# Row pairs 14 and 15 first in two of seven block products, their base kept in SBUF, and 40 accumulating DMAs spaced four products apart

## The chip, the cores and the metric

The kernel runs on one core of a Trainium2 chip. The core has a matrix engine (TensorE, PE in the profile, with its weight loads PEld), a vector engine (VectorE, DVE), a scalar engine (ScalarE, ACT), GpSimd (POOL) and a sync engine (SyncE, SP). In this kernel SP, ACT and POOL also issue DMAs. The metric is the device time of one execution in microseconds. Lower is better.

## The reference

The operation is a soft mixture of experts: every token goes through all eight experts, and the results are summed with the weights of a softmax.

```python
x [16, 512, 512]; router_logits [16, 512, 8]; expert_weights [8, 512, 2048]   # float32
probs = softmax(router_logits, axis=-1)
output = sum over e of probs[:, :, e:e+1] * (x @ expert_weights[e])           # [16, 512, 2048]
```

Seen as one matrix product, the left side has 8192 rows (tokens) and 4096 columns (expert times hidden, each already multiplied by its probability), and the right side is 4096 by 2048.

## The kernel before, in words

**Two levels of seven products.** The big product is cut 2 by 2 and done with seven block products P1 to P7 instead of eight (Winograd's form of Strassen's scheme). The 8192 rows are cut into 32 blocks of 256 rows. Row pair q (0 to 15) is the blocks 2q and 2q+1, one from each half of the scheme. For one row pair, one such product is 256 rows by 2048 by 1024, and it is again done by seven steps in the order 1, 5, 6, 2, 7, 3, 4 (`STEPS`), each of eight 128x128x512 matmuls. Some stages cut part of this a third time (`by_thirds`, `by_twos`), with 128x256 matmuls. The result of a product is four tiles of 128x512 float32, 256 KB each, named by (row half, column half).

**What is written where.** For row pair q the output has four blocks: C11 (even rows, left columns), C12 (even rows, right columns), C21 and C22 (odd rows).

- P1 goes to a DRAM scratch `kept[q]`. P2 goes to C11. For ten of the row pairs P1 is added onto C11 later by `add_kept`: four DMAs of 256 KB from `kept` to the output with an add, 40 in all, issued by POOL.
- P5 goes to C21. P6 starts from a base, P1 minus P5: `kept[q]` is fetched into SBUF tiles and P5's tiles are subtracted there (`joined`). P6 adds to the base in place and the tiles go to C12.
- P7 starts from what P6 left, adds in place, and goes to C22. Its base is fetched back from C12 in DRAM into SBUF (class `Base`, `fetch`, issued by SP).
- P4 starts from P7's tiles in SBUF and is added onto C21 by accumulating DMAs. P3 is added onto C12 in the same way.

All writes from a product's tiles to the output are DMAs issued by POOL (`pool`, line 121).

**The tiles that matter here.** Every 128x512 float32 tile outside PSUM comes from one pool, `hpool`, with 12 buffers (tiles named `h`). A new `h` tile takes the buffer whose last use in program order lies furthest back, and the first instruction that writes it waits until that use is over. If the last use is a write to the output, this means the landing of that DMA.

**Stages.** Work is listed in stages of one or two products, worked through step by step, alternating between the two: first product step 1, second product step 1, first product step 5, and so on. A stage of two has 14 slots. Stages 0 to 6 are P1, 7 to 14 are P2, 15 to 30 are P5 and P6, 31 (`k7`) is P6 of pair 15 with P7 of pair 0, 32 to 46 are P4 of pair q with P7 of pair q+1, 47 (`k3`) is P4 of pair 15 with P3 of pair 14, 48 to 54 are two P3 each and done by thirds, 55 is the last P3. `products[4, 15].apart` makes the last P4 write to new `h` tiles instead of in place.

**The order is written by hand.** Hooks `at(stage, slot, ...)` place loads, weight preparation, base fetches and `add_kept` at slots. Vector work that prepares later stages waits in a queue with costs, and a small planner (`slack`, `need`) takes it out between matmul groups. The resulting program order is kept on each engine, so an instruction that has to wait holds up all that follow on its engine or queue. POOL issues its DMAs in program order as well.

**Where the weights turn over.** Around stage 31 the weights of P4 and P7, around stage 47 the weights of P3 are fetched from DRAM scratch (`fetch_w`, issued by ACT, 1 MB each). From stage 47 on, P3 also loads a stored left side of 1 MB for each row pair (`ZBlock`, issued by SP).

The base fetches of P7 and the accumulating DMAs are placed by these lines:

```python
for slot, tn in zip((7, 9, 11, 17) if q else (10, 12, 14, 17), INNER):      # line 995, for each q
    fetch_at(k7 + q - 1 + slot // 14, slot % 14, bases[7, q], tn)
for n, q in enumerate(q for q in range(ON_BASE) if q not in WITH_KEPT):     # line 1246
    for i in range(4):
        at(*slots_after(k7 + 3, 0, 20 * n + 5 * i), lambda q=q, i=i: add_kept(q, i // 2, i % 2))
```

Of the kernel before, what the change touches and what calls it, by code (L numbers as in the profile page):

```python
# [31 lines left out]
def kernel(  # L32
# [87 lines left out]
    def pool(o, i, **how):  # L120
        note(nc.gpsimd.dma_start(out=o, in_=i, **how))  # L121
# [252 lines left out]
    def need(task):  # L374
        if task is not None and not task.done:
            flush(task)
            clock["pe"] = max(clock["pe"], clock["dve"])
# [275 lines left out]


    KEPT_Z = 14
    ND = 7
    ON_BASE = 14
    WITH_KEPT = (5, 1, 7, 9)

    def out_rows(q, odd, cols, tn):  # L660
        t, n = tn
        return out_f[ds((2 * q + odd) * HQ + t * HP, HP), ds(cols * NH + n * NB, NB)]

    def to_out(q, odd, cols, **how):
        return lambda tn, o: pool(out_rows(q, odd, cols, tn), o, **how)
# [14 lines left out]
    INNER = ((0, 0), (1, 1), (0, 1), (1, 0))  # L680
# [5 lines left out]
    def at(stage, slot, make):  # L686
        hooks.setdefault((stage, slot), []).append(make)

    def add(*products):
        stages.append(products)  # L690
        return len(stages) - 1
# [4 lines left out]
    lefts, xs, ps_, bases = {}, {}, {}, {}  # L696

    def xblock(h):
        if h not in xs:
            xs[h] = XBlock(h)  # L700
        return xs[h]

    def left_of(r, q, fresh=True):
        a, b = 2 * q, 2 * q + 1
        if r == 1:
            pt = PBlock(a, P1, xp1[q - 2][1] if q in (2, 3) else None)
            if q in (2, 3):
                xs[a] = XBlock(a, xp1[q - 2][0])
            return Left(xblock(a), pt), [xblock(a), pt]
        if r in (2, 4):  # L710
            h, pt = (a, PBlock(a, P2)) if r == 2 else (b, PBlock(b, P2))
            return Left(xblock(h), pt), [xblock(h), pt]
        if r == 5:
            pt = PBlock(b, PQ)
            return Left(xblock(b), pt), [xblock(b), pt]
        if r == 6:
            pt = PBlock(a, P1)
            return Left(xblock(a), pt, of=lefts[5, q]), [xblock(a), pt]
        if r == 3 and q < KEPT_Z:
            pt, kept_z = PBlock(a, P2), ZBlock(q)  # L720
            return Left(xblock(a), pt, kept=kept_z), [xblock(a), pt, kept_z]
        pa, pb = PBlock(a, P1 if r == 7 else PQ), PBlock(b, P1 if r == 7 else PQ)
        return Left(xblock(a), pa, (xblock(b), pb)), [xblock(a), pa, xblock(b), pb]

    def kept_rows(q):
        return lambda tn: kept[q][tn[1], ds(tn[0] * HP, HP), :]

    def product(r, q, **how):
        left, loads = left_of(r, q)
        lefts[r, q] = left  # L730
        p = None
        if r == 1:
            def sink(tn, o):
                pool(kept_rows(q)(tn), o)
            p = Product(right[1], left, sink)
        elif r == 2:
            if q >= ON_BASE or q in WITH_KEPT:
                bases[2, q] = Base(kept_rows(q))
            p = Product(right[2], left, to_out(q, 0, 0), bases.get((2, q)))
        elif r == 5:  # L740
            bases[6, q] = m1 = Base(kept_rows(q))
            m1.task = {}

            p = Product(right[5], left, to_out(q, 1, 0))
        elif r == 6:
            m1 = bases[6, q]

            def base(tn):
                need(m1.task[tn])
                return m1.t[tn]  # L750
            p = Product(right[6], left, to_out(q, 0, 1), base)
        elif r == 7:
            base = bases[7, q] = Base(lambda tn: out_rows(q, 0, 1, tn))
            p = Product(right[7], left, to_out(q, 1, 1), base)
        elif r == 4:
            p = Product(right[4], left, to_out(q, 1, 0, accum_op=ADD), products[7, q].o.__getitem__)
        else:
            p = Product(right[3], left, to_out(q, 0, 1, accum_op=ADD), **how)
        p.loads = loads
        products[r, q] = p  # L760
        return p

    products = {}
# [179 lines left out]
    def fetch_at(stage, slot, base, *tns):  # L943
        for tn in tns:
            at(stage, slot, lambda tn=tn: base.fetch(tn))


    for q in range(2, 16, 2):
        add(product(1, q), product(1, q + 1))
    xs.clear()  # L950
    for q in (2, 4, 0, 6, 8, 10, 12, 14):
        add(product(2, q), product(2, q + 1))
    for q in (*WITH_KEPT, *range(ON_BASE, 16)):
# [3 lines left out]
        fetch_at(k, 3, bases[2, q], INNER[3])  # L957
    xs.clear()
    k5 = add(product(5, 0), product(5, 1))
    add(product(6, 0))  # L960
    for q in range(1, 15):
        add(product(6, q), product(5, q + 1))
    some = product(6, 15)
    xs.clear()
    k7 = add(some, product(7, 0))
    for q in range(15):
        add(product(4, q), product(7, q + 1))
    some = product(4, 15)
    xs.clear()
    k3 = add(some, product(3, KEPT_Z))  # L970
    for q in range(0, KEPT_Z, 2):
        add(product(3, q), product(3, q + 1))
# [1 line left out]
    late[k3 - 1] = 6  # L974
    late[k3] = 10
    late[k7] = 12
    products[4, 15].apart = True

    def claim(of, tn):
        of[tn] = half()  # L980
# [2 lines left out]
    def joined(q, tn):  # L983
        m1 = bases[6, q]
        m1.task[tn] = later(0.69, lambda: tt(m1.t[tn], m1.t[tn], products[5, q].o[tn], SUB), True)

    for q in range(16):
        k = k5 + 1 + q
        duo = len(stages[k - 1]) == 2
        for slot, tn in zip((2, 4, 6, 8) if duo else (1, 2, 3, 4), INNER):  # L990
            fetch_at(k - 1, slot, bases[6, q], tn)
        for tn, where in zip(INNER, ((k - 1, 12), (k - 1, 13), (k - 1, 13), (k, 3)) if duo
                             else ((k - 1, 5), (k - 1, 6), (k - 1, 6), (k, 3))):
            at(*where, lambda q=q, tn=tn: joined(q, tn))
        for slot, tn in zip((7, 9, 11, 17) if q else (10, 12, 14, 17), INNER):
            fetch_at(k7 + q - 1 + slot // 14, slot % 14, bases[7, q], tn)


    def wedge(kn, e):

# [26 lines left out]
    def wedge_at(stage, slot, kn, e, then):  # L1027
        made = []

        def begin():  # L1030
            casts, made_ = wedge(kn, e)
            casts()
            made.extend(made_)

        def go_on():
            for make in made:
                later(1.22, make)
        at(stage, slot, begin)
        at(*then, go_on)
# [9 lines left out]
    def sums_at(stage, slot, r, of, ps, first=False):  # L1049
        def go():  # L1050
            if right[r].w is None:
                right[r].sums = right[r].build(of)
            for p in ps:
                right[r].queue_sum(right[r].sums, p, first)
        at(stage, slot, go)
    sums_at(ND - 1, 5, 2, b21, (5,))
    sums_at(ND - 1, 7, 2, b21, (6,))
    sums_at(ND - 1, 9, 2, b21, (7,))
    sums_at(ND - 1, 12, 2, b21, (4,))
    ODD = 0, 1  # L1060
    for i, (kn, e) in enumerate((kn, e) for kn in (ODD, (0, 0), (1, 1), (1, 0)) for e in range(2)):
        stage = ND + i - 2 if kn != ODD else 2 + 2 * i
        wedge_at(stage, 2, kn, e, (stage + 1, 0))
# [41 lines left out]
    def slots_after(stage, slot, n):  # L1105
        slot += n
        while slot >= 7 * len(stages[stage]):
            slot -= 7 * len(stages[stage])
            stage += 1
        return stage, slot  # L1110
# [97 lines left out]

    for q in range(KEPT_Z):
        z_dram[q] = dram.tile([P, 2 * K8, HQ], f16, name=f"z_{q}")  # L1210
# [15 lines left out]
    def third_at(stage, slot, of, r, p):  # L1226
        def make():
            of[p] = third_sums(right[r].w[p])
        at(stage, slot, lambda: later(2.76, make))
    third_at(1, 5, third, 1, 2)  # L1230
    for stage in range(2, ND - 1):
        twos[stage] = Twos(*(p.left for p in stages[stage]), third)
# [10 lines left out]
    def add_kept(q, n, t):  # L1243
        pool(out_f[ds(2 * q * HQ + t * HP, HP), ds(n * NB, NB)], kept[q][n, ds(t * HP, HP), :], accum_op=ADD)

    for n, q in enumerate(q for q in range(ON_BASE) if q not in WITH_KEPT):
        for i in range(4):
            at(*slots_after(k7 + 3, 0, 20 * n + 5 * i), lambda q=q, i=i: add_kept(q, i // 2, i % 2))

    finish = products[3, 15]  # L1250
    finish.base = Base(lambda tn: out_rows(15, 0, 1, tn))
# [81 lines left out]
```

## Time and profile before

| what | value |
|---|---|
| median of 3 runs | 1365.92 us (1365.02 to 1368.73) |
| the profiled execution's own time | 1368.37 us |
| its span, first to last instruction | 1366.6 us |
| PE busy | 1352.8 us (99%) |
| DVE busy | 1156.6 us (85%) |
| ACT busy, POOL busy | 254.0 us, 422.3 us |
| DMAs `out_dram<-h` (results to the output, POOL) | 380 of 256 KB |
| DMAs `out_dram<-kept` (P1 onto C11, POOL) | 40 of 256 KB |
| DMAs `h<-out_dram` (bases read back, SP) | 68 of 256 KB |

How to read it: tiles are named by what they hold, `ps` and `pt` are PSUM banks, `h` the 128x512 float32 tiles, `w` the weights and the stored left sides, `z` and `d` left sides. `out_dram<-h` means a transfer or instruction that writes `out_dram` and reads `h`. Line L121 is the helper that issues POOL's DMAs, L118 that of SP, L130 the matmul helper, L107 the helper of all two-input vector operations, so tiles tell more than lines. L624, L628, L632, L645 and L831 to L847 are ScalarE copies out of PSUM. A busy PE is not PE at its peak: when the granted clock (PEclk) is 0.50, matmuls take twice as long and still count as busy.

### The profile page before, as it was taken

How to read it: one execution, taken by the hardware profiler on the slowest of the kernel's cores; microseconds unless marked ns; L12 is line 12 of the kernel's file. 1: busy time of each engine (PE TensorE's matmuls, PEld its weight loads, DVE VectorE, ACT ScalarE, POOL GpSimd, SP SyncE). 2: the span in 40 equal slices, each digit the busy share in tenths (PEclk: the TensorE clock that was granted, in tenths of full speed). 3: DMA queues.
4: the chain of work that ended last, by engine and by line, in shares of the span. 5: the costliest groups of instructions: out<-in, count | busy, mean ns of one | idle time of the engine just before them, and what ended most of it. 6: DMA issues, size and time to landing. Idle time of an engine off the chain costs nothing.

```text
span 1366.6 us, 18926 instructions
## 1 busy us (share of the span) xinstructions
PE 1352.8 (99%) x6894; PEld 672.1 (49%) x6894; DVE 1156.6 (85%) x1426; ACT 254.0 (19%) x517; POOL 422.3 (31%) x651
## 2 busy tenths in 40 slices
PE   9999999999999999999999999999999999989998
PEld 4566655565544444444444444444444444546564
DVE  7878898888999888887878899898888987868886
ACT  3233323232211111111111100000000000223331
POOL 3223322323222323223221122433534433232232
PEclk9999999999999999999999999999999999999999
DMA  9999979998999999999987997999999999999986
GB/s 184 245 216 242 263 244 233 307 297 258 272 321 280 304 296 284 280 272 308 290 276 278 361 305 196 279 233 260 238 240 239 274 243 309 325 276 220 209 130 119
DMA packets 191117, 355.67 MB, mean 260 GB/s; under 512 B 53040, under 2 KB 81968, under 8 KB 186160
## 3 DMA queue, kind: packets, MB, share of 16 engines
q0 software_dynamic: 87520, 185.12, 57.9%
q1 hardware_dynamic: 99760, 144.05, 34.5%
q10 hardware_dynamic: 3744, 25.30, 4.7%
q8 instruction: 54, 0.88, 0.3%
q14 instruction: 39, 0.32, 0.1%
HBM read 210.53 MB, written 176.36 MB: 283 GB/s over the span
## 4 chain that ended last, share of the span: by engine, by line
PE 77%; issue 10%; DMA 8%; POOL 3%; DVE 1%; ACT 0%; POOLq 0%; DVEq 0%; SPq 0%; ACTq 0%
PE ps L130 59%; PE pt L130 18%; DMA out_dram<-h 4%; POOL out_dram L121 2%; DMA w<-in_expert_weights_dram 1%; DMA out_dram<-kept 1%; DMA h<-out_dram 1%; DMA wd<-w 1%; POOL wd L121 0%; DVE h L107 0%; DVE z L107 0%; DVE w L107 0%; POOL w L121 0%; POOL xs L121 0%; DVE u L107 0%
## 5 line engine op out<-in xcount | busy, mean ns | idle before, releaser
L130 PE MATMUL ps<-w,z 128*128 128x512 f16 (+1 forms) x3728 | 811.5, 374 | 2.1 <-DVE h L107 0.9
L130 PEld LDWEIGHTS <-z 128*128 128x128 f16 x5312 | 520.0, 98 | 572.5 <-issue 2.6
L121 POOL DMA_DIRECT2D out_dram<-h x380 | 251.2, 687 | 702.0 <-ACT h L645 282.6
L130 PE MATMUL pt<-w,z 128*128 128x512 f16 (+1 forms) x1584 | 325.6, 352 | 0.3 <-DMA w<-in_expert_weights_dram 0.3
L107 DVE TENSOR_TENSOR z<-xT,pT 128x2048 f16<-128x2048 f16 x220 | 265.6, 1216 | 0.8 <-DMA xT<-xs 0.8
L107 DVE TENSOR_TENSOR h<-ps,h 128x512 f32<-128x512 f32 x270 | 183.9, 687 | 79.1 <-PE ps L130 60.7
L130 PE MATMUL ps<-w,d 128*128 128x512 f16 x880 | 199.7, 379 | 0.0
L130 PEld LDWEIGHTS <-d 128*128 128x128 f16 x880 | 86.1, 98 | 98.9
L632 ACT COPY h<-ps 128x512 f32<-128x512 f32 x102 | 59.8, 586 | 396.8 <-PE ps L130 359.5
L107 DVE TENSOR_TENSOR z<-z,d 128x2048 f16<-128x2048 f16 x110 | 132.3, 1216 | 0.0
L107 DVE TENSOR_TENSOR h<-pt,h 128x512 f32<-128x512 f32 x123 | 83.5, 686 | 43.5 <-PE pt L130 41.6
L107 DVE TENSOR_TENSOR w<-w 128x1024 f16<-128x1024 f16 (+2 forms) x108 | 112.7, 1059 | 0.8
L645 ACT COPY h<-ps 128x512 f32<-128x512 f32 x54 | 31.7, 586 | 398.5 <-PE ps L130 397.4
L107 DVE TENSOR_TENSOR d<-z 128x1024 f16<-128x1024 f16 x110 | 73.9, 684 | 0.9
L628 ACT COPY h<-ps 128x512 f32<-128x512 f32 x89 | 50.0, 598 | 76.7 <-PE ps L130 74.6
L107 DVE TENSOR_TENSOR ps<-ps,h 128x512 f32<-128x512 f32 (+1 forms) x70 | 44.3, 636 | 21.5 <-PE ps L130 16.0
L121 POOL DMA_DIRECT2D kept<-h x56 | 30.7, 548 | 87.0 <-DVE h L107 48.0
L624 ACT COPY ps<-ps 128x512 f32<-128x512 f32 x47 | 26.8, 570 | 110.4 <-PE ps L130 51.0
L107 DVE TENSOR_TENSOR z<-z 128x2048 f16<-128x2048 f16 (+1 forms) x48 | 45.6, 957 | 1.4
L107 DVE TENSOR_TENSOR h<-h 128x512 f32<-128x512 f32 (+2 forms) x69 | 45.1, 674 | 1.1 <-DMA h<-kept 0.9
L107 DVE TENSOR_TENSOR z<-z,u 128x2048 f16<-128x2048 f16 x36 | 44.1, 1225 | 1.2
L107 DVE TENSOR_TENSOR u<-xT,pT 128x2048 f16<-128x2048 f16 x36 | 43.8, 1217 | 0.0
(83 smaller groups left out, 553.8 us busy)
## 6 DMA issues: line engine op xcount, KB each, us to landing
out_dram<-h POOLq DMA_DIRECT2D x380, 256.0 KB, 7.2
pT<-p_dram SPq DMA_DIRECT2D x126, 256.0 KB, 7.2
w<-wd ACTq DMA_DIRECT2D x23, 1024.0 KB, 10.2
h<-kept SPq DMA_DIRECT2D x88, 256.0 KB, 7.4
xT<-x SPq DMA_DIRECT2D x80, 256.0 KB, 7.1
h<-out_dram SPq DMA_DIRECT2D x68, 256.0 KB, 5.9
w<-in_expert_weights_dram POOLq DMA_DIRECT2D x33, 512.0 KB, 11.0
kept<-h POOLq DMA_DIRECT2D x56, 256.0 KB, 6.8
```

The lines of the kernel that those rows point to most:

```text
L107: dve(nc.vector.tensor_tensor(out=o, in0=a, in1=b, op=op))
L121: note(nc.gpsimd.dma_start(out=o, in_=i, **how))
L130: note(nc.tensor.matmul(ps, z, w, start=start, stop=stop, skip_group_check=True))
L624: act(nc.scalar.copy(self.banks["b"], x))
L628: act(nc.scalar.copy(o[tn], q if p == 5 else x))
L632: act(nc.scalar.copy(o[TN[p]], b if p == 2 else x))
L645: act(nc.scalar.copy(o[tn], b))
```

## The change

Three things change.

1. P7 and P4 take the row pairs in the order 14, 15, 0, 1, ..., 13 instead of 0 to 15. Stage 31 is now P6 of pair 15 with P7 of pair 14, stage 32 P4 of pair 14 with P7 of pair 15, stage 33 P4 of pair 15 with P7 of pair 0, and stage 47 P4 of pair 13 with P3 of pair 14.
2. For pairs 14 and 15, P7 takes P6's own four tiles in SBUF as its base and adds to them in place. The eight fetches from C12 that would bring these bases are gone. The other 14 pairs fetch their base as before, at the same slots before their use. The four special slots that pair 0 had (10, 12, 14, 17) are gone.
3. The 40 accumulating DMAs of `add_kept` begin at the same place (stage 34, slot 0) and follow each other 4 slots apart instead of 5. The last one is at slot 156 counted from there (stage 45, slot 2) instead of slot 195 (stage 47, slot 13).

```diff
+    ORDER_7 = (14, 15, *range(14))
...
         elif r == 7:
-            base = bases[7, q] = Base(lambda tn: out_rows(q, 0, 1, tn))
+            base = products[6, q].o.__getitem__
+            if q not in ORDER_7[:2]:
+                base = bases[7, q] = Base(lambda tn: out_rows(q, 0, 1, tn))
...
-    k7 = add(some, product(7, 0))
-    for q in range(15):
-        add(product(4, q), product(7, q + 1))
-    some = product(4, 15)
+    k7 = add(some, product(7, ORDER_7[0]))
+    for q, then in zip(ORDER_7, ORDER_7[1:]):
+        add(product(4, q), product(7, then))
+    some = product(4, ORDER_7[-1])
...
-    products[4, 15].apart = True
+    products[4, ORDER_7[-1]].apart = True
...
-        for slot, tn in zip((7, 9, 11, 17) if q else (10, 12, 14, 17), INNER):
-            fetch_at(k7 + q - 1 + slot // 14, slot % 14, bases[7, q], tn)
-
+    for n, q in enumerate(ORDER_7[2:], 2):
+        for slot, tn in zip((7, 9, 11, 17), INNER):
+            fetch_at(k7 + n - 1 + slot // 14, slot % 14, bases[7, q], tn)
...
-            at(*slots_after(k7 + 3, 0, 20 * n + 5 * i), lambda q=q, i=i: add_kept(q, i // 2, i % 2))
+            at(*slots_after(k7 + 3, 0, 16 * n + 4 * i), lambda q=q, i=i: add_kept(q, i // 2, i % 2))
```

## The prediction, written before the changed kernel was run

> **What bounds the kernel now.** I read the busy times first, then who PE waits for, then the stages in which it waits, and last what ends those waits.
>
> ```profile
> span 1366.6 us, 18926 instructions
> PE 1352.8 (99%) x6894; PEld 672.1 (49%) x6894; DVE 1156.6 (85%) x1426; ACT 254.0 (19%) x517; POOL 422.3 (31%) x651
> ```
>
> PE is busy 99% of the span and the change leaves every matmul in place. So time can only come from PE's idle gaps and from matmuls run at a lower clock, or be lost to new gaps. The waits of PE:
>
> ```profile
> PE pt L130 <- ACT h L835: 4.3, 1, 4.3
> ...
> PE ps L130 <- DVE h L107: 0.9, 1, 0.9
> PE ps L130 <- ACT h L628: 0.7, 1, 0.7
> PE ps L130 <- DVE z L107: 0.5, 1, 0.5
> PE pt L130 <- ACT ps L831: 0.4, 1, 0.4
> ```
>
> The waits left out here belong to the kernel's first microseconds, which the change does not touch. The stages in which the five fall, one row per stage (window, its length, then busy time per engine, the granted clock, the DMA share and GB/s):
>
> ```profile
> 766.48:791.74 25.26, 24.35 (x113) 10.92 (x112) 21.63 (x24) 1.76 (x3) 3.78 (x7) 1.00 0.98 368
> 791.74:816.38 24.64, 24.17 (x113) 10.82 (x112) 23.65 (x28) 1.17 (x2) 5.37 (x9) 1.00 0.85 271
> 816.38:1106.40 290.02, 290.02 (x1345) 131.46 (x1344) 258.08 (x308) 14.07 (x24) 114.38 (x161) 1.00 0.98 247
> 1179.17:1203.93 24.76, 23.70 (x137) 13.29 (x136) 20.24 (x26) 8.16 (x18) 6.62 (x9) 1.00 1.08 302
> 1203.93:1233.49 29.56, 25.21 (x137) 14.17 (x136) 19.71 (x25) 8.04 (x18) 10.34 (x13) 0.94 1.09 256
> 1233.49:1256.87 23.38, 23.38 (x137) 13.29 (x136) 19.64 (x25) 8.23 (x18) 6.84 (x9) 1.00 1.00 228
> 1212.29:1215.71 3.42, 3.42 (x19) 2.44 (x17) 0.87 (x2) 0.85 (x2) 0.53 (x1) 0.50 1.06 252
> ```
>
> The first two rows are stages 31 and 32, where P7 begins: PE idles 25.26 - 24.35 = 0.91 us and 24.64 - 24.17 = 0.47 us. The third is stages 33 to 44: no idle time at all. The fourth and fifth are stages 48 and 49, the first two of P3, the sixth is stage 50, undisturbed. The last row shows that after the gap of 4.35 us PE ran 3.42 us at half clock, which costs another 1.71 us.
>
> **The gap in stage 49.** The timeline of PE and the chain of waits there:
>
> ```profile
> 1207.00 0.60 PE L130 MATMUL pt<-w 128*128 128x256 f16 x4
> 1211.94 0.71 PE L130 MATMUL pt<-w 128*128 128x256 f16 x4 [4.35 <-ACT h L835]
> ```
>
> ```profile
> 1189.31 22.13 DMA out_dram<-h
> ...
> 1211.52 0.38 ACT h L835
> ```
>
> PE waits for a ScalarE copy, and the copy waits for a buffer of `h`, which a write to the output holds: issued at 1189.31, landed 22.13 us later. In calmer stretches such a write takes a third of that. The DMA issues by stretch (count, size, median time to landing), first 835 to 1110 us, then 1125 to 1215, then 1221 to 1310; the row with three times is minimum, median and maximum of POOL's writes to the output in that stretch:
>
> ```profile
> out_dram<-h POOLq DMA_DIRECT2D x94, 256.0 KB, 7.7
> h<-out_dram SPq DMA_DIRECT2D x44, 256.0 KB, 6.4
> out_dram<-kept POOLq DMA_DIRECT2D x33, 256.0 KB, 8.2
> DMA to landing us min/median/max: 4.6/7.8/10.6
> ```
>
> ```profile
> w<-z SPq DMA_DIRECT2D x8, 1024.0 KB, 14.0
> out_dram<-h POOLq DMA_DIRECT2D x30, 256.0 KB, 18.7
> w<-wd ACTq DMA_DIRECT2D x6, 1024.0 KB, 13.3
> out_dram<-kept POOLq DMA_DIRECT2D x7, 256.0 KB, 19.5
> ```
>
> ```profile
> out_dram<-h POOLq DMA_DIRECT2D x32, 256.0 KB, 6.7
> w<-z SPq DMA_DIRECT2D x5, 1024.0 KB, 9.1
> ```
>
> So POOL's queue is backlogged in the turnover to P3 alone, where fourteen loads of 1 MB and seven of the accumulations from `kept` meet.
>
> **The gaps in stages 31 and 32.** VectorE's waits from 740 to 820 us, the sync queue from 757 us, and the chain:
>
> ```profile
> DVE ps L107 <- DMA h<-out_dram: 2.9, 1, 2.9
> ...
> DVE h L107 <- DMA h<-out_dram: 1.9, 2, 1.3
> ```
>
> ```profile
> 757.73 19.02 SPq L118 DMA_DIRECT2D h<-out_dram  x7
> ```
>
> ```profile
> 755.47 7.15 DMA out_dram<-h
> ...
> 762.66 15.05 DMA h<-out_dram
> ```
>
> The base fetches of P7's first pair need buffers that P6's writes have to free (7.15 us), then take up to 15.05 us, and keep the sync queue for 19.02 us. VectorE loses 2.9 us and more to them, in stages where it is busy 21.63 of 25.26 and 23.65 of 24.64 us, and PE then waits for it.
>
> **The change part by part.**
>
> *Eight base fetches go (pairs 14 and 15).* The waits of VectorE on them go, and with them PE's 0.91 and 0.47 us: 1.38 us. Bounds: 0, if VectorE is late for its own load, and 1.38. I take 1.38, since the 2.9 us that it gets back are more than PE's gaps. Next late there is the first fetch that stays, for stage 33; it finds buffers freed earlier than now (P5's last tiles), because the eight tiles are not allocated.
>
> *A wait is added:* P7 of these two pairs overwrites P6's tiles, and has to wait until their writes to the output land. A slot is 290.02 / 168 = 1.73 us (12 stages of 14 slots). P6 finishes its tile (1,1) in slot 8, and P7 first writes it in slot 3 of the next stage, 9 slots or 15.5 us later; (0,1) has 9 as well, the others more. POOL's writes from 740 to 800 us take at most 11.1 us:
>
> ```profile
> DMA to landing us min/median/max: 2.6/8.8/11.1
> ```
>
> With the copy out of PSUM before it this is 13 us at worst, so I cost it at nothing. Behind it on VectorE stand copies out of PSUM and left sides, for which PE would wait; its upper bound is what the fetches cost today, 1.38 us. From P7 to P4 the same reuse exists already with 7 slots.
>
> *The order of the pairs* swaps equal work: each stage has the same loads of `xT` and `pT` on SP, the same writes on POOL, the same vector work. No P4 or P3 accumulation comes closer than two stages to the write it adds to, so no DMA waits anew. 0 us.
>
> *The accumulations, 4 slots apart.* The last is issued at stage 45, slot 2, about 1110 us, instead of:
>
> ```profile
> L121 POOL DMA_DIRECT2D out_dram<-kept x40: 823/892/1303, 844.9 to 1187.1; - x40
> ```
>
> Seven leave the stretch from 1125 to 1215 us. That stretch lands 37 of POOL's output DMAs in 90 us, 2.43 us each; only those issued from 1150 us on surely stand ahead of the write that PE waits for:
>
> ```profile
> out_dram<-kept POOLq DMA_DIRECT2D x4, 256.0 KB, 22.8
> ```
>
> That is 4 x 2.43 = 9.7 us at least, and 7 x 2.43 = 17.0 us at most. Landing 9.7 us earlier is more than twice the gap of 4.35 us. So I expect the gap, the half clock behind it (1.71) and the gaps of 0.37 and 0.69 us in stage 48, which hang on the same buffers, to go: 7.12 us. Bounds: 0, if the 1 MB loads alone make the backlog, and 24.76 + 29.56 - 2 x 23.38 = 7.56 us, what the two stages are longer than stage 50. 7.12 is the sum of named gaps and near the upper end, because the margin is twofold.
>
> The seven go into the 290 us from 816 to 1106 us, one per 6.9 us instead of per 8.6. POOL has room (114 of 290 us busy, each issue about 0.9 us), and a product's write behind one comes that much later. The landing there is 7.7 us at the median and 10.6 at most, P7 to P4 allows 7 slots, 12.1 us, and VectorE has 32 us of slack. 0 us, with an upper bound under the rivals.
>
> [...]
>
> **The sum.** 1.38 + 7.12 = 8.50 us. Against the profiled execution, 1368.37 us (span 1366.6 and 1.77 around it), this gives 1359.87. The median of the runs is 2.45 us lower than that execution. If unprofiled executions have that much less of these gaps, the gain over the median is 6.05 and the time 1359.9; if not, it is 8.50 and 1357.4. I take 1359.0, nearer to the first, because runs that differ by 3.7 us with the same matmuls differ in gaps.
>
> **Rivals.**
>
> *The backlog stays.* Fourteen loads of 1 MB make it and seven small DMAs do not matter. For it: these loads are slow there too (14.0 against 9.1 us). Against it: from 1221 to 1310 us, with five such loads and no accumulation, writes land in 6.7 us. Then only stages 31 and 32 gain: 1365.92 - 1.38 = 1364.5. If half of the gain comes, 1361 to 1362. [...]
>
> *Slower: the denser accumulations spill over.* The DMA share is 0.98 in the third row already. If the engines have no room there, seven more cost 7 x 2.43 = 17.0 us of the queue, writes land later, P4 waits for P7's tiles, and VectorE (258.08 of 290.02 us busy) hands it on to PE. It decides from landings over 12.1 us on; at most 17.0 - 8.5 = 8.5 us are lost, 1374.4. Against it: the share is 1.00 in stage 50 too, without a gap, and the maximum now is 10.6 us. [...]
>
> *The base in SBUF trades one wait for another.* The write of P6 lands late, VectorE waits as long as now, 1.38 us stay: 1360.4.
>
> **How the numbers follow.** A measurement here tells about 0.3%, 4.1 us, from no change. Both gaps go (1357 to 1361.5): 0.60. The base trades its wait: 0.08. The backlog stays or shrinks too little (1361.8 to 1365): 0.18. Slower by spilling over: 0.14. So faster 0.68, same 0.18, slower 0.14. The range from 1356.8 to 1364.8 leaves out the slower case and little below; for the likeliest alone it is 1357 to 1361.5.
>
> **What the new profile would show.** Right: `out_dram<-kept` ends near 1110 us, writes from 1125 to 1215 us land in 8 to 13 us at the median, stages 48 and 49 last 23.4 us at clock 1.00, `h<-out_dram` counts 60, stages 31 and 32 have no gap. Wrong: landings near 19 us there (first rival), gaps of PE with VectorE behind `out_dram<-h` between 816 and 1130 us (second), or VectorE waiting for `out_dram<-h` in stages 31 and 32 (third).

## The result, and the profile after

The changed kernel takes 1359.40 us at the median of 5 runs (1358.97 to 1360.59); the kernel before took 1366.84 us at the median of its 5 runs (1365.02 to 1368.73). The ratio is 0.9948 with a 95% interval of 0.9933 to 0.9962: faster by half a per cent, clear of the noise. The forecast was 1359.0. The profiled execution of the changed kernel took 1359.61 us, where the sum against the profiled execution before had given 1359.87.

The page of the changed kernel begins, and its chain of work that ended last reads:

```profile
span 1357.9 us, 18909 instructions
PE 1350.9 (99%) x6894; PEld 671.5 (49%) x6894; DVE 1157.0 (85%) x1426; ACT 254.4 (19%) x517; POOL 423.5 (31%) x651
...
PE 99%; DMA 1%; POOL 0%; issue 0%; ACT 0%; POOLq 0%
```

PE alone makes the chain now. The stages that answer to those of the prediction (31, 32, 33 to 44, then 48, 49 and 50; columns as there):

```profile
766.48:790.65 24.17, 24.17 (x114) 10.93 (x113) 22.22 (x24) 1.76 (x3) 4.34 (x8) 1.00 0.98 379
790.65:814.82 24.17, 24.17 (x114) 10.97 (x112) 22.49 (x28) 1.17 (x2) 4.89 (x8) 1.00 0.78 219
814.82:1104.86 290.04, 290.04 (x1345) 131.52 (x1344) 258.65 (x308) 14.09 (x24) 121.70 (x168) 1.00 1.00 252
...
1177.40:1200.80 23.40, 23.40 (x138) 13.32 (x136) 20.28 (x26) 8.24 (x18) 6.92 (x9) 1.00 1.07 301
1200.80:1224.20 23.40, 23.40 (x138) 13.32 (x137) 19.66 (x25) 8.24 (x18) 6.92 (x8) 1.00 1.07 284
1224.20:1247.60 23.40, 23.40 (x138) 13.33 (x137) 19.66 (x25) 8.24 (x18) 6.96 (x9) 1.00 1.03 225
```

No stage has a gap, and the granted clock is 1.00 in all of them. By stage length, 31 and 32 gave 25.26 + 24.64 - 2 x 24.17 = 1.56 us, and 48 and 49 gave 24.76 + 29.56 - 2 x 23.40 = 7.52 us. The 290 us between keep no gap either, though the accumulations are denser there.

The DMA issues of the changed kernel (count, size, median to landing), with the minimum, median and maximum for POOL's writes to the output: first from 835 to 1110 us, then from 1125 to 1215 us. The last row is over the whole span.

```profile
out_dram<-h POOLq DMA_DIRECT2D x94, 256.0 KB, 8.0
...
out_dram<-kept POOLq DMA_DIRECT2D x40, 256.0 KB, 8.2
...
DMA to landing us min/median/max: 4.9/8.1/11.3
```

```profile
w<-z SPq DMA_DIRECT2D x9, 1024.0 KB, 13.3
out_dram<-h POOLq DMA_DIRECT2D x31, 256.0 KB, 12.0
w<-wd ACTq DMA_DIRECT2D x6, 1024.0 KB, 9.8
...
DMA to landing us min/median/max: 5.3/12.0/19.2
```

```profile
h<-out_dram SPq DMA_DIRECT2D x60, 256.0 KB, 6.8
```

All 40 accumulations now land between the turnovers, for 0.3 us more at the median of the other writes there (8.0 instead of 7.7). In the turnover to P3 the writes still land late, 12.0 us at the median and 19.2 at most, but not late enough to stop anybody.

### The profile page after: what moved, and what is told of

Its sections match the earlier page's. It is cut to its first block, busy times and chain, and to the rows that moved or that the text cites. A ratio compares the mean times of both kernels' runs of the same rounds, so it can differ in the third digit from the quotient of the medians.

```text
span 1357.9 us, 18909 instructions
## 1 busy us (share of the span) xinstructions
PE 1350.9 (99%) x6894; PEld 671.5 (49%) x6894; DVE 1157.0 (85%) x1426; ACT 254.4 (19%) x517; POOL 423.5 (31%) x651
## 4 chain that ended last, share of the span: by engine, by line
PE 99%; DMA 1%; POOL 0%; issue 0%; ACT 0%; POOLq 0%
PE ps L130 74%; PE pt L130 25%; DMA w<-in_expert_weights_dram 1%; POOL w L121 0%; ACT h L1282 0%; POOL ident L225 0%; POOLq L225 0%; POOLq L1320 0%
## 5 line engine op out<-in xcount | busy, mean ns | idle before, releaser
L121 POOL DMA_DIRECT2D out_dram<-h x380 | 254.8, 693 | 692.0 <-ACT h L645 288.5
L107 DVE TENSOR_TENSOR ps<-ps,h 128x512 f32<-128x512 f32 (+1 forms) x70 | 44.3, 636 | 17.3 <-PE ps L130 14.8
## 6 DMA issues: line engine op xcount, KB each, us to landing
w<-in_expert_weights_dram POOLq DMA_DIRECT2D x33, 512.0 KB, 11.1
```

Source lines behind the costliest of these rows:

```text
L107: dve(nc.vector.tensor_tensor(out=o, in0=a, in1=b, op=op))
```

## The experiments

Theory A is that of the prediction: two parts that act apart, the SBUF base in stages 31 and 32, the spacing of the accumulations in stages 48 and 49. Theory B is its first rival: the 1 MB loads make the backlog, and a gain there would come from something else. Ratios are to the kernel before on the same chip.

### One part at a time

**The spacing alone:** the kernel before, with one line of the change.

```diff
-            at(*slots_after(k7 + 3, 0, 20 * n + 5 * i), ...)
+            at(*slots_after(k7 + 3, 0, 16 * n + 4 * i), ...)
```

> The kernel before with one part of the change: the accumulations 4 slots apart; order and base fetches as before. Theory A (the two parts act apart, spacing frees the turnover to P3, the SBUF base frees stages 31 and 32): the gaps of stages 48 and 49 are gone, those of stages 31 and 32 stay (about 1.4 us); span about 1359.3 us, time 1360 to 1361. Theory B (the 1 MB loads make the backlog and the gain in stage 49 came with the new order and its eight DMAs fewer): the gap of about 4 us in stage 49 and the half clock stay, time 1366 to 1367.

Measured: 1359.67 us (1359.34 to 1361.14, 5 runs), ratio 0.9952 (0.9939 to 0.9964), just under A's 1360 to 1361. Stages 48 and 49 have no gap: A holds there and B falls. The surprise is in stages 31 and 32, where this execution has no gap either. The two stages by windows, and VectorE's waits from 740 to 820 us:

```profile
766.48:790.65 24.17, 24.17 (x114) 10.93 (x113) 21.61 (x24) 1.76 (x3) 4.33 (x8) 1.00 1.02 377
790.65:814.82 24.17, 24.17 (x114) 10.97 (x113) 22.93 (x28) 1.18 (x2) 4.96 (x8) 1.00 0.92 292
```

```profile
DVE ps L107 <- DMA h<-out_dram: 2.6, 1, 2.6
...
DVE h L107 <- DMA h<-out_dram: 1.0, 1, 1.0
```

VectorE waits for the base fetches as before, a little less (before: 2.9 and, in stages 31 to 33 together, 1.9 us, and 0.9 us for a fetch from `kept`), and in this execution PE does not wait at all.

**The order and the SBUF base alone:** the changed kernel with the old spacing.

```diff
-            at(*slots_after(k7 + 3, 0, 16 * n + 4 * i), ...)
+            at(*slots_after(k7 + 3, 0, 20 * n + 5 * i), ...)
```

> The changed kernel with its accumulations 5 slots apart again: only the order and the base in SBUF are changed. Theory A: no gap in stages 31 and 32, writes to the output from 1125 to 1215 us land in about 18 us at the median, the gap in stage 49 stays with 3.4 us of half clock; time 1364.5 to 1366, a gain of about 1.4 us. Theory B: no gap in stage 49, time 1359 to 1361.

Measured: 1364.66 us (1363.27 to 1367.54, 11 runs), ratio 0.9987 (0.9978 to 0.9996). No gap in stages 31 and 32, and the gap in stage 49 stays, as A says. PE's waits in the turnover to P3:

```profile
PE pt L130 <- ACT h L838: 3.1, 1, 3.1
...
PE ps L130 <- DVE z L107: 0.8, 1, 0.8
```

The gap of 3.1 us had no half clock behind it in this execution, see the last section.

**What the base is worth once the spacing is 4.** The changed kernel and the spacing alone, on one chip. First the changed kernel:

> The changed kernel itself, beside the next one on the same chip: what the new order with the base in SBUF is worth once the spacing is 4. Theory A (1.38 us of gaps in stages 31 and 32 are there in each execution without it): this one 1.2 to 1.5 us faster than the next. Rival, after one execution with spacing alone showed no gap there (those gaps stand only in some executions, when VectorE loses over about 3 us): 0.1 to 0.8 us faster.

> The kernel before with the accumulations 4 slots apart alone, order and base fetches as before, on the same chip as the changed kernel. Theory A: 1.2 to 1.5 us slower than the changed kernel, gaps of 0.9 and 0.5 us in stages 31 and 32. Rival: 0.1 to 0.8 us slower, gaps there in some executions only.

Measured: 1359.21 us (1358.98 to 1360.19, 5 runs; ratio 0.9954, 0.9941 to 0.9966) for the changed kernel, 1360.36 us (1359.23 to 1361.23, 5 runs; ratio 0.9961, 0.9948 to 0.9973) for the spacing alone. The medians are 1.15 us apart, just under what A expected, but the runs and the intervals overlap, and against the first five runs of the changed kernel the spacing alone was only 0.3 us behind. This time its profiled execution had gaps in stages 31 and 32, of 0.41 and 0.48 us:

```profile
766.48:791.14 24.66, 24.25 (x114) 10.91 (x112) 20.73 (x24) 1.76 (x3) 3.73 (x7) 1.00 0.99 373
791.14:815.80 24.66, 24.18 (x113) 10.81 (x112) 23.67 (x28) 1.17 (x2) 4.94 (x9) 1.00 0.83 274
```

So these gaps are there in some executions and not in others, between 0 and 1.4 us; what sets their size from one execution to the next is not shown. The 1.15 us lie outside the rival's range (0.1 to 0.8 us) as well as A's; what is shown is that the gap varies.

**The order without the SBUF base:** the changed kernel, with the first two pairs fetching from C12 as well.

```diff
-            base = products[6, q].o.__getitem__
-            if q not in ORDER_7[:2]:
-                base = bases[7, q] = Base(lambda tn: out_rows(q, 0, 1, tn))
+            base = bases[7, q] = Base(lambda tn: out_rows(q, 0, 1, tn))
...
-    for n, q in enumerate(ORDER_7[2:], 2):
-        for slot, tn in zip((7, 9, 11, 17), INNER):
+    for n, q in enumerate(ORDER_7):
+        for slot, tn in zip((7, 9, 11, 17) if n else (10, 12, 14, 17), INNER):
```

> The changed kernel, but pairs 14 and 15 fetch their base from DRAM too (the first pair at the slots that pair 0 had before). Theory A (the base in SBUF makes the gain in stages 31 and 32, the order alone makes none): the fetches must now wait for P6's writes to land, VectorE waits for them, gaps of 1.4 us or more come back in stages 31 and 32, time 1360.5 to 1364. Rival (the order alone, or the special slots taken away, makes the gain): no gap there, time as the changed kernel, 1359.4.

Measured: 1360.96 us (1360.29 to 1362.27, 4 runs), ratio 0.9960 (0.9944 to 0.9975). The gaps are back, 0.76 and 0.47 us, a little less than the 1.4 us that A named:

```profile
PE ps L130 <- DVE h L107: 0.8, 1, 0.8
...
PE ps L130 <- DVE z L107: 0.5, 1, 0.5
```

The order alone gains nothing (the spacing alone took 1359.67 us); it is what makes P6's tiles still be there when P7 wants them.

### Where the accumulations fall

**Three stages earlier, still 5 apart:** the kernel before with one edit.

```diff
-            at(*slots_after(k7 + 3, 0, 20 * n + 5 * i), ...)
+            at(*slots_after(k7, 0, 20 * n + 5 * i), ...)
```

> The kernel before with only the start of the accumulations moved from stage 34 to stage 31, still 5 slots apart, so that the last is issued at stage 44, slot 13. Theory A (what counts is that none falls into the turnover to P3): stages 48 and 49 have no gap, as with 4 slots apart; the gaps in stages 31 and 32 stay or grow by up to 1 us, since three accumulations per stage now meet that turnover; time 1360 to 1362. Rival (the closer spacing itself matters, not the place): the gap in stage 49 stays, time 1366 to 1367.

Measured: 1367.32 us (1366.9 to 1369.09, 10 runs), ratio 1.0010 (1.0001 to 1.0019): a miss. The gaps in stages 48 and 49 are gone as A says, so it is the place, not the spacing. But a larger one opened at the other turnover. PE and VectorE:

```profile
811.60 5.78 PE L130 MATMUL ps<-w,z 128*128 128x512 f16 x16 [4.68 <-DVE z L107]
```

```profile
809.12 1.29 DVE L107 TENSOR_TENSOR h<-ps,h 128x512 f32<-128x512 f32 x2 [6.68 <-DMA out_dram<-h]
```

A vector add waits 6.68 us for a write to land before it may overwrite the tile (in this stage these are P4's adds into P7's tiles), PE loses 4.68 us, and goes on slower: the 16 matmuls behind the gap take 5.78 us, where the 16 before it take 3.62. This is the mechanism of the slower rival, in a place where the prediction had not put it.

**Two and three stages later, 4 apart:** the changed kernel with `k7 + 5`, and with `k7 + 6`, in place of `k7 + 3`.

> The changed kernel, spacing 4 as in it, but all 40 accumulations two stages later (from stage 36, the last at stage 47, slot 2), so that some four fall into the turnover to P3 again. Theory A (it is their place in that turnover that makes the late landings): landings from 1125 to 1215 us rise from 12.0 us to 14 to 18 at the median, part of the idle time in stages 48 and 49 comes back, 0.5 to 4 us, time 1360 to 1364. Rival (the gain came from the spacing or from eight fetches fewer, whatever the place): no gap, time 1359.4.

> The changed kernel with all 40 accumulations three stages later (from stage 37, the last at stage 48, slot 2, about 1184 us). With the last at 1159.6 us the landings were as late as before (18.9 us at the median) and PE had lost only 0.37 us; with the last at 1187.1 us (the kernel before) 5.4 us and the half clock. Theory A in its narrower form (only accumulations that stand ahead of the write which the buffer of stage 49 waits for cost time, those issued after about 1160 us): the gaps in stages 48 and 49 come back, 2 to 8 us, time 1362 to 1368. Rival (with the base in SBUF or the new spacing the turnover bears them): no gap over 1 us, 1359 to 1361.

Measured: two stages later 1359.97 us (1359.54 to 1360.25, 4 runs), ratio 0.9949 (0.9934 to 0.9964); three stages later 1365.37 us (1364.63 to 1367.69, 10 runs), ratio 0.9999 (0.9990 to 1.0008). Two stages later: when the accumulations are issued, and the landings of POOL's writes from 1125 to 1215 us.

```profile
L121 POOL DMA_DIRECT2D out_dram<-kept x40: 805/888/1473, 889.9 to 1159.6; - x40
...
DMA to landing us min/median/max: 6.7/18.5/25.5
```

Three stages later, the same two rows, and PE's gaps in the turnover:

```profile
L121 POOL DMA_DIRECT2D out_dram<-kept x40: 810/888/1198, 913.2 to 1192.8; - x40
...
DMA to landing us min/median/max: 9.4/18.7/25.6
```

```profile
1191.20 1.89 PE L130 MATMUL ps<-w,z 128*128 128x512 f16 x8 [0.48 <-ACT h L628]
1195.65 4.65 PE L130 MATMUL ps<-w,z 128*128 128x512 f16 x13 [2.57 <-ACT h L628]
```

Both kernels land writes as late as the kernel before did (18.8 us at the median), with six and nine accumulations issued from 1125 to 1215 us. In the first PE idles 0.37 us in the turnover; in the second it idles 4.08 us in four gaps, of which the rows show the two longest together, and then runs 3.41 us at half clock. For theory A the first was a miss, just outside its three ranges (landings of 14 to 18 us, gaps of 0.5 to 4 us, 1360 to 1364 us). For its narrower form the second was a hit.

Why does the median tell so little? In the trace before, as in the one after, none of POOL's DMAs starts before the one eight places ahead of it has landed (638 such pairs in each, the closest start 0.28 us after that landing). From 1125 to 1215 us the time to landing, counted from the issue, hardly differs between these three kernels (18.8, 18.5 and 18.7 us at the median, 25.5, 25.5 and 25.6 at most); what differs is the time that POOL waits for that landing before it issues. In this stretch it waited so 13 times, 23.2 us in all, in the kernel before, 7 times (13.1 us) two stages later, 15 times (34.5 us) three stages later, and never in the changed kernel.

The write whose buffer stage 49 waits for shows what that does. In the kernel before it was issued at 1189.31 us and landed at 1211.44. In the changed kernel it was issued at 1179.15 and landed 17.3 us later, at 1196.4: 15.0 us earlier, two thirds of it by the earlier issue. Two stages later it was issued at 1183.32 and took 20.9 us, to 1204.2; the ScalarE copy that needs its buffer, and starts when the matmuls before it are done, stands at 1204.39:

```profile
1183.32 0.86 POOL L121 DMA_DIRECT2D out_dram<-h  x1 [1.95 <-DMA out_dram<-h]
...
DMA to landing us min/median/max: 20.9/20.9/20.9
...
1204.39 0.37 ACT L838 COPY h<-pt 128x256 f32<-128x256 f32 x1
```

So accumulations issued up to 1159.6 us are not free: they made this write land 7.8 us later than in the changed kernel, and it was in time by 0.2 us. Those issued later, three in the kernel before, carry it over that edge. How late the last one may be, between 1159.6 and 1185 us, was not tried.

### How dense they may be

The changed kernel with the accumulations 3, 2 and 1 slots apart, and without any.

```diff
-            at(*slots_after(k7 + 3, 0, 16 * n + 4 * i), ...)
+            at(*slots_after(k7 + 3, 0, 12 * n + 3 * i), ...)     # 3 apart; 8 * n + 2 * i; 4 * n + i
```

> The changed kernel with its accumulations 3 slots apart (4.7 in each stage, the last at stage 42, slot 5). Between 4 apart (no wait of VectorE for writes, maximum landing 11.3 us) and 2 apart (27.6 us of waits, maximum 18.3). Theory A, as it stands after those runs (the distance P7 to P4 of 12.1 us decides, by the latest landings and not the median): landings from 816 to 1040 us reach 11 to 14 us at most, waits of VectorE of 0 to 3 us in total, no or small gaps, time 1359 to 1361. Rival (VectorE and the queue have no room at all over 4 apart): a third or half of what 2 apart loses, 1363 to 1367.

> The changed kernel with its accumulations 2 slots apart: 7 in each stage of 24.2 us, the last at stage 39, slot 8. Theory A (there is room on POOL's queue and the engines between the turnovers; lateness decides only from the distance P7 to P4, 12.1 us, on): landings from 816 to 960 us rise to 9 to 12 us, no gap, time 1359 to 1361. Rival (the transfer engines are full there, so that denser means later at once): VectorE waits for writes, gaps of PE behind it, 2 to 15 us slower than the changed kernel.

> The changed kernel with its accumulations 1 slot apart: 14 in each stage of 24.2 us, the last at stage 36, slot 11. With 8 writes of results, 22 of POOL's DMAs at 2.4 us each would be 53 us for a stage of 24. Theory A: here the distance of 12.1 us is passed, landings go over 15 us, VectorE waits for P7's writes, PE for VectorE, with half clock after long gaps: 3 to 25 us slower than the changed kernel. Rival (the cost of an accumulation is much less than 2.4 us of the queue outside the turnover): no gap, time as the changed kernel.

> The changed kernel without the 40 accumulations of P1 onto C11: that part of the sum is left out, so this is no complete computation. Theory A (at 4 slots apart they are hidden in full): no gain, 1359 to 1360; landings from 835 to 1110 us fall from 8.1 to about 6 us; landings in the turnover stay near 12 us, which is then the share of the 1 MB loads alone. Rival (the accumulations still cost time somewhere): faster than the changed kernel by over 1 us.

| apart | time, us | ratio (95% interval) | VectorE waits for writes, 740 to 1110 us | latest landing, 835 to 1110 us |
|---|---|---|---|---|
| none at all | 1358.93 (4 runs) | 0.9944 (0.9929 to 0.9958) | 1.0 us in 1 | 8.5 us |
| 4 (the change) | 1359.21 (5 runs) | 0.9954 (0.9941 to 0.9966) | none | 12.6 us |
| 3 | 1359.90 (4 runs) | 0.9958 (0.9942 to 0.9973) | 8.2 us in 6 | 14.7 us |
| 2 | 1373.24 (10 runs) | 1.0047 (1.0032 to 1.0062) | 27.6 us in 9 | 18.3 us |
| 1 | 1391.76 (4 runs) | 1.0186 (1.0170 to 1.0203) | 27.4 us in 5 | 18.2 us |

The rows behind it, VectorE's waits and the landings from 835 to 1110 us, for 3 apart, then for 2 apart with PE's wait, then for 1 apart:

```profile
DVE h L107 <- DMA out_dram<-h: 8.2, 6, 2.5
...
DMA to landing us min/median/max: 4.4/8.9/14.7
```

```profile
PE ps L130 <- DVE h L107: 10.3, 6, 3.9
...
DVE h L107 <- DMA out_dram<-h: 27.6, 9, 6.4
...
DMA to landing us min/median/max: 4.1/10.2/18.3
```

```profile
PE ps L130 <- DVE h L107: 25.6, 5, 10.6
...
DVE h L107 <- DMA out_dram<-h: 27.4, 5, 13.0
```

At 4 apart the accumulations are hidden: leaving them out altogether gains 0.3 us between medians of runs on two chips, less than the intervals can tell. At 3 apart VectorE waits six times and hides nearly all of it; PE loses one gap of 0.56 us. The time is in A's range, the waits (0 to 3 us expected) and the latest landing (11 to 14 us) are above theirs. At 2 apart the waits are longer than VectorE can make up for, and the kernel is slower than before the change. So the expectation for 2 apart was a miss: the rival held there, although the median landing was as A had it (11.0 us from 816 to 960 us). At 1 apart A named the direction, but 32 us against the changed kernel is more than its 3 to 25.

The time to landing does not tell 2 apart from 1 apart: the latest takes 18.3 and 18.2 us, while PE loses 10.3 and 25.6 us. Here too POOL's wait before the issue has to be added. VectorE's longest wait at 1 apart ended on a write that landed only 11.7 us after its issue, but POOL had waited 3.13 us for an earlier DMA before it issued it:

```profile
938.24 0.58 POOL L121 DMA_DIRECT2D out_dram<-h  x1 [3.13 <-DMA out_dram<-kept]
```

```profile
950.05 0.69 DVE L107 TENSOR_TENSOR h<-pt,h 128x512 f32<-128x512 f32 x1 [12.96 <-DMA out_dram<-h]
```

Without any accumulation the writes from 1125 to 1215 us still land in 12.3 us at the median, as in the changed kernel:

```profile
out_dram<-h POOLq DMA_DIRECT2D x30, 256.0 KB, 12.3
```

Against 6.2 to 6.7 us in the calmer stretch behind it, where five such loads run instead of fifteen, some 6 us are the share of the 1 MB loads; the accumulations added another 6 to 7. The first rival was right that the loads slow POOL's queue, and wrong that the accumulations do not matter.

## Why the prediction was right

**The turnover to P3 (7.12 us): right.** The stages gave 7.52 us in the profile; over runs, the spacing alone gained 6.5 and 5.4 us between medians. The profiled execution before stood 2.45 us over the median then known, and the prediction took this for gaps larger than most; the result, 1359.4 rather than 1357.4, fits that. That the forecast of 1359.0 came within 0.4 us is in part luck: the median of the kernel before moved from 1365.92 us with 3 runs to 1366.84 with 5. The proof for the mechanism is that the gaps go with the spacing alone and come back when the accumulations are put behind 1160 us, whatever their spacing.

**Its margin: right.** The prediction had the write that PE waits for land 9.7 to 17.0 us earlier, against a gap of 4.35 us. It landed 15.0 us earlier. What the prediction did not say is that most of this is an earlier issue, and not a shorter time to landing. The loads' share of the lateness, left as a rival, is real, but it is half (some 6 of 12 us over the calmer stretch).

**The eight fetches (1.38 us): right cause, the size is that of one execution.** VectorE's waits on the fetches are gone and so are PE's gaps. But the same stages, with the fetches in place, had gaps of 1.38 us (twice, the second time beside the 4.68 us of the accumulations three stages earlier), 1.23, 0.89 and 0 us in five profiled executions, and between medians the base was worth 0.3 to 1.15 us on top of the spacing, and 1.5 us without it. The prediction had bounds of 0 and 1.38 and took the upper end.

**The added wait of P7 for P6's writes (0 us): right.** In the changed kernel VectorE has no wait for `out_dram<-h` between 740 and 1110 us, although these writes took up to 13.5 us from 740 to 800 us instead of 11.1; the reuse distance of 15.5 us covers that.

**The denser accumulations (0 us): right at 4 slots, and close; the threshold was not.** VectorE has no waits for writes at 4, 8.2 us at 3, 27.6 us at 2, and PE follows between 3 and 2 (0.56 us of gaps behind VectorE, then 10.3). The prediction named the path rightly (P4's adds wait for P7's writes, and VectorE hands the wait on to PE), but "landings over 12.1 us" does not decide: at 4 apart the latest landing of 12.6 us stopped nobody, with the start three stages earlier VectorE waited although no landing from 835 to 1110 us took over 11.3, and at 1 apart it waited longest for a write that took 11.7. The term left out is POOL's wait before the issue. The bound of 8.5 us of loss held for seven more accumulations in the same stretch; at 1 apart the kernel lost 25 us against the kernel before. The risk at the first turnover, seen three stages earlier, was not named.

**The order (0 us): right.** With bases from DRAM the new order is no faster than the spacing alone.

## What to carry to other kernels

When PE is busy 99%, read its few gaps one by one and follow each to the buffer and the DMA that frees it. Small background DMAs that nobody waits for can still hold up the buffers of the writes issued behind them: here the write that PE waited for landed 15.0 us earlier without them, and the gap of 4.35 us was gone. Place them away from bursts of large loads. Set the whole time from the finished tile to the landing of its write against the distance at which the buffer is used again: the time to landing counts from the issue and leaves out the wait before it (23.2 us in the turnover before), and its median says little (18.5 us with 0.37 us of idle PE, 18.7 with 4.08). A result that is still in SBUF is a better base than the same result fetched back, if the order of the work can be turned so that it is used next (here worth 0.3 to 1.5 us between medians).

## What the runs showed of the hardware that was not expected

In these runs a gap's length alone does not tell whether the half clock follows. With the base alone changed, PE idled 3.11 us and went on at full clock; in the kernel three stages later, it idled 2.57 us and then ran 3.41 us at 0.50. The gap and the stretch behind it, first for the base alone, then for three stages later (the window rows: length, busy PE, PEld, DVE, ACT, POOL, granted clock, DMA share, GB/s):

```profile
1208.74 0.60 PE L130 MATMUL pt<-w 128*128 128x256 f16 x4 [3.11 <-ACT h L838]
```

```profile
1208.74:1212.20 3.46, 3.46 (x28) 2.73 (x28) 1.88 (x4) 1.63 (x5) 0.86 (x1) 1.00 1.09 191
```

```profile
1192.53:1195.94 3.41, 0.84 (x5) 0.33 (x4) 1.35 (x2) 0.59 (x1) 0.83 (x1) 1.00 1.04 335
1195.94:1199.35 3.41, 3.41 (x10) 1.23 (x9) 0.28 (x1) 0.59 (x1) 0.07 (x1) 0.50 1.08 265
```

In the second kernel the 3.41 us just before the clock fell held 0.84 us of PE work and 2.57 us of idle time. What decides between the two cases was not measured.
